# Dealing 24 modulation columns out among weight units, and reordering the opening of a two-layer decoder trunk

## Chip, cores and metric

One core of a Trainium2 chip runs the whole kernel. The metric is the device time of one execution in microseconds; where several were timed, the median is given.

## The reference, cut to what matters

A decoder trunk of two layers on one sequence of 1024 tokens, width 1024. Every layer takes six modulation vectors from the same condition: shift, scale and gate of the mixing half, shift, scale and gate of the MLP half.

```python
cond = jax.nn.silu(c)
for l in range(DEPTH):
    mod = cond @ w_mod[l] + b_mod[l]
    sh1, sc1, gt1, sh2, sc2, gt2 = [m[:, None, :] for m in jnp.split(mod, N_MOD, axis=-1)]
    h = rms_norm(x, norm_g[l, 0]) * (1.0 + sc1) + sh1
    y = mixer_block(h, positions, w_in[l], ...)
    x = x + gt1 * rms_norm(y, norm_g[l, 1])
    h = rms_norm(x, norm_g[l, 2]) * (1.0 + sc2) + sh2
    y = jnp.square(jax.nn.relu(h @ w_up[l])) @ w_down[l]
    x = x + gt2 * rms_norm(y, norm_g[l, 3])
```

`mixer_block` multiplies h by one input projection (2716 columns), feeds four mixers of width 256 from it (a short gated convolution, attention with a compressed, a full and a windowed branch, gated linear attention, a causal spatial gate over chunks of 128), norms each, and multiplies the four results by w_o. All matrices are fp32. Attention rotates 16 of its 64 dimensions by angles from `positions`.

## The kernel before, in words

Activations lie with features on the 128 partitions and 512 tokens along a tile, so a 1024-wide vector is eight tiles and the sequence is two halves (`hf` 0 and 1). A matrix product of fp32 is made of three TensorE matmuls at fp32r precision: weights and activations are each split into a high part (a cast, on ScalarE) and a low part (raw minus high, on VectorE: `sub`, L131), and `mm3` (L173 to L175) adds high by high, high by low, low by high into PSUM. A gemm (`gemm`) of one 128-wide output block is 24 such matmuls in two units of 12; `wunit` loads a unit's 256 KB (`wraw`, L158), casts it (L167) and subtracts (L131). Lanes are sets of buffers for this: "a" for w_o and the mixers, "b" for the second stream of the first half's mixing, "f" for the MLP. Lane "b" has three raw buffers of 256 KB and four for parts, so two units.

Work is ordered by a planner: the block is built with a scheduler that walks a simulated timeline, hands out buffers of a tag in turn, and gives each engine a fixed list; what comes earlier in the program has the higher priority, except where `tc.high_priority` moves it by an offset (the ones matmul of a norm, L195, forward). At run time every engine and every DMA-issuing queue takes its list in order. All loads and stores are issued by SyncE (SP).

Modulation vectors are not made by TensorE. `w_mod` is stored transposed, 128 outputs by 1024 inputs for each of 48 tiles of a layer; the condition is copied to all partitions (`cond`, 128x1024), and VectorE multiplies and sums along the row: `mod_dot` (L239) with a whole tile of 512 KB, `mod_half` (L247) with two halves of 256 KB and a small step that adds them and the bias. A column (j, k) is one such tile: modulation j, features 128k to 128k+127.

The opening (`start`) comes first: the rotary tables (`rope_tables`, tables of cosine and sine made with a chain of small VectorE steps, eight transposes and four matmuls, L380, and stored to DRAM), the condition's silu (L289 to L292), the loads of x, its norm factor R (`rms_R`: squares on ScalarE, L188 and L191, sums on VectorE, L137, one ones matmul, L195, then logarithm and exponential, L199 and L200), and then for each of eight k: columns (0, k) and (1, k), the tile of h (`make_h`: x by A1 and by R on VectorE, shift and cast on ScalarE, L209, low part on VectorE), and its 18 matmuls into six PSUM banks for the six input blocks `EARLY` (gates, compressed, full and window keys and values, queries). The six blocks' weights come in two halves (`wload` L277, `wsplit` L282), into a pool `kw` of their own.

`mix(0, 0)` then has its own order: a pool "wb" for lane "b", opened there; gates; attention (`nsa_part`) on lane "a"; linear attention (six gemms on lane "b"), spatial gate (four), convolution (six); then `mods_now`, which makes the 24 columns of modulations 2, 3 and 4 of layer 0 through lane "b"'s raw buffers; then attention's group norm, the split of the eight outputs, and the w_o gemms on lane "a" (`yo` copied by ScalarE, L946), beside which the second half's `norm` (its `make_h`) is made. Modulation 2 is needed by the residual after w_o, 3 and 4 by the next norm.

## Time and profile before

| | |
|---|---|
| median of 3 runs (lowest to highest) | 2634.32 us (2633.39 to 2635.1) |
| the profiled execution | 2634.88 us, span 2633.1 us |
| TensorE busy | 2488.4 us, 95% |
| VectorE busy | 1631.0 us, 62% |
| ScalarE busy | 1310.5 us, 50% |
| GpSimd busy | 53.0 us, 2% |
| granted TensorE clock, mean | 0.975 |
| moved by DMA | 305.79 MB, 116 GB/s |

Times of the profile count from the span's start. An engine is busy while an instruction runs on it; matmuls overlap, so a matmul's own duration is longer than its share of the queue. The granted clock is the share of TensorE's full clock that the chip allowed. "idle before <-releaser" tells how long an engine stood before an instruction and what it waited for last. DVE is VectorE, ACT ScalarE, POOL GpSimd, PE TensorE, PEld its weight loads, SP and SPq SyncE and its queue.

### The profile page before, as it was taken

To read this page: it belongs to the slowest core of one execution; us is meant where nothing else is said; L and a number is where in the kernel's file an instruction comes from. 1 tells how busy PE (TensorE), PEld (TensorE's weight loads), DVE (VectorE), ACT (ScalarE), POOL (GpSimd) and SP (SyncE) were. 2 spreads that over 40 slices of the span, in tenths; PEclk is the share of its full clock that TensorE was granted. 3 is DMA by queue.
4 is the path that set the end of the run, shared out by engine and by line. 5 is a ranking of instruction groups with operands and counts; after the bars stand their busy time and mean duration, and the time that the engine had idled before them with its cause. 6 is when DMAs were issued, how large, how long until landed. Compare 5 with 4: busy or idle time off the path is not lost.

```text
span 2633.1 us, 34406 instructions
## 1 busy us (share of the span) xinstructions
PE 2488.4 (95%) x11834; PEld 1987.3 (75%) x11834; DVE 1631.0 (62%) x3425; ACT 1310.5 (50%) x2657; POOL 53.0 (2%) x65
## 2 busy tenths in 40 slices
PE   5899499999999999999999999999999998899997
PEld 3666277777877878887787878877788876788886
DVE  7676866557888577444676476544567755634445
ACT  3573345445665356344366445444466744443333
POOL 0100000000000000000100000000100000000000
PEclk9899699999999999999999999999999999999999
DMA  8313634345434454322522344322322134433332
GB/s 279 100 46 100 203 117 132 106 140 153 129 123 134 155 164 140 102 85 89 154 83 70 116 152 140 99 84 79 119 77 68 57 108 143 136 97 96 97 97 75
DMA packets 176200, 305.79 MB, mean 116 GB/s; under 512 B 21573, under 2 KB 33434, under 8 KB 176026
## 3 DMA queue, kind: packets, MB, share of 16 engines
q1 hardware_dynamic: 176026, 303.60, 36.7%
q8 instruction: 93, 1.52, 0.2%
q14 instruction: 81, 0.66, 0.1%
HBM read 281.50 MB, written 17.83 MB: 114 GB/s over the span
## 4 chain that ended last, share of the span: by engine, by line
PE 83%; DVE 6%; DMA 4%; issue 1%; ACT 1%; POOL 0%; DVEq 0%; SPq 0%; ACTq 0%; POOLq 0%
PE ps_ff L173 16%; PE ps_ff L174 16%; PE ps_ff L175 16%; PE ps_mm L173 8%; PE ps_mm L175 8%; PE ps_mm L174 8%; DMA raw_f<-in_w_mod_dram 2%; PE ps_pv L783 1%; PE ps_mm L777 1%; PE ps_pv L782 1%; PE ps_s L822 1%; DMA raw_b<-in_w_mod_dram 1%; PE ps_s L824 1%; PE ps_t L777 1%; PE ps_t L195 1%
## 5 line engine op out<-in xcount | busy, mean ns | idle before, releaser
L167 ACT CAST w_f<-raw_f 128x512 fp32r<-128x512 f32 x504 | 311.7, 619 | 426.3 <-PE ps_ff L174 409.2
L131 DVE TENSOR_TENSOR w_f<-raw_f,w_f 128x512 fp32r<-128x512 f32 x504 | 350.4, 696 | 178.7 <-ACT w_f L167 167.9
L173 PE MATMUL ps_ff<-hid,w_f 128*128 128x512 f32 x992 | 395.4, 399 | 21.7 <-DVE yf L137 12.7
L175 PE MATMUL ps_ff<-h,w_f 128*128 128x512 f32 x1024 | 405.4, 396 | 1.2 <-DVE w_f L131 1.2
L173 PE MATMUL ps_ff<-h,w_f 128*128 128x512 f32 x1024 | 403.1, 394 | 0.0
L174 PE MATMUL ps_ff<-h,w_f 128*128 128x512 f32 x1024 | 402.3, 393 | 0.0
L174 PE MATMUL ps_ff<-hid,w_f 128*128 128x512 f32 x992 | 392.4, 396 | 1.5 <-DVE hid L131 1.5
L175 PE MATMUL ps_ff<-hid,w_f 128*128 128x512 f32 x992 | 391.7, 395 | 0.0
L173 PE MATMUL ps_mm<-h,w_a 128*128 128x512 f32 x784 | 318.2, 406 | 32.6 <-ACT yo L946 23.7
L175 PE MATMUL ps_mm<-h,w_a 128*128 128x512 f32 x784 | 317.2, 405 | 6.0 <-DVE w_a L131 6.0
L174 PE MATMUL ps_mm<-h,w_a 128*128 128x512 f32 x784 | 314.8, 403 | 3.6 <-DVE h L131 3.6
L167 ACT CAST w_a<-raw_a 128x512 fp32r<-128x512 f32 x196 | 121.3, 620 | 304.5 <-PE ps_mm L174 278.7
L131 DVE TENSOR_TENSOR w_a<-raw_a,w_a 128x512 fp32r<-128x512 f32 x196 | 135.1, 689 | 179.2 <-ACT w_a L167 173.3
L173 PEld LDWEIGHTS ps_ff<-hid,w_f 128*128 128x128 f32 x992 | 188.1, 190 | 69.8 <-DVE yf L137 15.2
L175 PEld LDWEIGHTS ps_ff<-h,w_f 128*128 128x128 f32 x1024 | 192.3, 188 | 45.5 <-issue 2.9
L173 PEld LDWEIGHTS ps_ff<-h,w_f 128*128 128x128 f32 x1024 | 192.4, 188 | 43.0 <-issue 3.1
L174 PEld LDWEIGHTS ps_ff<-h,w_f 128*128 128x128 f32 x1024 | 192.4, 188 | 42.0 <-issue 2.2
L174 PEld LDWEIGHTS ps_ff<-hid,w_f 128*128 128x128 f32 x992 | 188.3, 190 | 44.6 <-issue 2.9
L175 PEld LDWEIGHTS ps_ff<-hid,w_f 128*128 128x128 f32 x992 | 187.9, 189 | 41.1 <-issue 1.4
L137 DVE TENSOR_TENSOR y<-y,ps_ff 128x512 f32<-128x512 f32 (+1 forms) x208 | 138.0, 664 | 125.0 <-PE ps_ff L175 123.8
L173 PEld LDWEIGHTS ps_mm<-h,w_a 128*128 128x128 f32 x784 | 149.9, 191 | 72.8 <-ACT yo L946 24.1
L175 PEld LDWEIGHTS ps_mm<-h,w_a 128*128 128x128 f32 x784 | 149.8, 191 | 44.5 <-DVE w_a L131 7.7
(390 smaller groups left out, 3610.2 us busy)
## 6 DMA issues: line engine op xcount, KB each, us to landing
raw_f<-in_w_up_dram SPq DMA_DIRECT2D x256, 256.0 KB, 2.7
raw_f<-in_w_down_dram SPq DMA_DIRECT2D x256, 256.0 KB, 2.7
raw_a<-in_w_in_dram SPq DMA_DIRECT2D x132, 256.0 KB, 2.6
raw_f<-in_w_mod_dram SPq DMA_DIRECT2D x112, 256.0 KB, 2.9
raw_a<-in_w_o_dram SPq DMA_DIRECT2D x64, 256.0 KB, 2.7
raw_b<-in_w_mod_dram SPq DMA_DIRECT2D x48, 256.0 KB, 3.1
mw<-in_w_mod_dram SPq DMA_DIRECT2D x16, 512.0 KB, 5.7
bp<-in_cmp_w_dram SPq DMA_DIRECT2D x32, 256.0 KB, 5.7
```

The lines of the kernel that those rows point to most:

```text
L131: V.tensor_tensor(out=out, in0=a, in1=b, op=ALU.subtract)
L137: eng.tensor_tensor(out=out, in0=a, in1=b, op=ALU.add)
L167: A.copy(hi, raw)
L173: PE.matmul(ps_ap, wh, xh, start=start, stop=False)
L174: PE.matmul(ps_ap, wh, xl, start=False, stop=False)
L175: PE.matmul(ps_ap, wl, xh, start=False, stop=stop)
L195: PE.matmul(p, ones, acc, start=True, stop=True)
L777: PE.transpose(tp[0:kn, hh, :], cols(h0 + hh), ident)
L782: PE.matmul(pv[:, h0:h0 + nh, :], vst, th[0:kn], start=first[0], stop=False)
L783: PE.matmul(pv[:, h0:h0 + nh, :], vst, tl[0:kn], start=False, stop=last)
L822: PE.matmul(sp[:, 0:w], qh[:, h0 + hh, :], KX[:, 128 * k0:128 * k0 + w], start=True, stop=False)
L824: PE.matmul(sp[:, 0:w], ql[:, h0 + hh, :], KX[:, 128 * k0:128 * k0 + w], start=False, stop=True)
```

## The change

It has two parts. First, the 24 columns of modulations 2, 4 and 3 are taken out of their block behind the convolution: a generator yields one column after each weight unit of lane "b", and lane "b"'s pool is opened before `start`. Second, `start` is reordered: condition first, parameters and table inputs loaded from GpSimd's queue, first `w_mod` tiles ahead of x, six `w_mod` buffers instead of four, the sum of squares made by eight accumulating ones matmuls, x multiplied by R on GpSimd, scale and shift in one ScalarE step followed by a cast and a subtraction, the low parts of the early weights made on GpSimd and held in the ring of h tiles, the second half's early weights loaded at k = 1 and split at k = 3, and the rotary tables' arithmetic last, with another PSUM bank.

```diff
@@ -104,10 +104,10 @@
             d[name] = const.tile(shape, F32, name=f"{name}{l}")
         par.append(d)
 
-    def load_params(l, names):
+    def load_params(l, names, load=dma):
         src = {"ng": norm_g, "bmod": b_mod, "conv": conv_w, "gain": gains}
         for n in names:
-            dma(out=par[l][n], in_=src[n][l])
+            load(out=par[l][n], in_=src[n][l])
 
 
     KS = const.tile([128, 1024], F32R, name="KS")
@@ -169,6 +169,8 @@
         sub(lo, raw, hi.bitcast(F32))
         return hi, lo
 
+    beside = {}
+
     def mm3(ps_ap, wh, wl, xh, xl, start, stop):
         PE.matmul(ps_ap, wh, xh, start=start, stop=False)
         PE.matmul(ps_ap, wh, xl, start=False, stop=False)
@@ -177,6 +179,8 @@
     def gemm(ps_ap, lane, src, h, order=(0, 1, 2, 3, 4, 5, 6, 7)):
         for kh in (order[0] // 4, order[4] // 4):
             hi, lo = wunit(lane, src[:, 4 * kh:4 * kh + 4, :], [128, 4, 128])
+            if lane in beside:
+                next(beside[lane], None)
             for kk in order:
                 if kk // 4 == kh:
                     k = kk % 4
@@ -200,9 +204,9 @@
         A.activation(R, R, AF.Exp, scale=-0.5)
         return R
 
-    def make_h(xt, R, Ac, shc, ks=range(8)):
+    def make_h(xt, R, Ac, shc):
         h = []
-        for k in ks:
+        for k in range(8):
             t = nt()
             stt(t, xt[k], Ac[:, k:k + 1], R, ALU.mult, ALU.mult)
             hi, lo = htile(), htile()
@@ -265,10 +269,9 @@
     def start():
         d = par[0]
         early = {}
-        rope_tables()
-        with region("kw", "right") as kw, region("su") as su:
+        with region("kw", "right") as kw, region("rp") as rp, region("su") as su:
             def mk(src, shape):
-                t = su.tile(shape, F32, name="mw", tag="mw", bufs=4)
+                t = su.tile(shape, F32, name="mw", tag="mw", bufs=6)
                 dma(out=t, in_=src)
                 return t
 
@@ -278,48 +281,73 @@
                 return raw
 
             def wsplit(raw):
-                hi, lo = (kw.tile([128, 4, 128], F32R, name="w_k", tag="w_k", bufs=12) for _ in range(2))
+                hi, lo = (hp.tile([128, 4, 128], F32R, name="w_k", tag="h", bufs=32) for _ in range(2))
                 A.copy(hi, raw)
-                sub(lo, raw, hi.bitcast(F32))
+                P.tensor_tensor(out=lo, in0=raw, in1=hi.bitcast(F32), op=ALU.subtract)
                 return hi, lo
 
-            for hf in range(2):
+            def mload(k):
+                return [mk(w_mod[0, 8 * j + k], [128, 1024]) for j in (0, 1)]
+
+            halves = [slice(hf * T, hf * T + T) for hf in range(2)]
+            for c_ in halves:
+                dma(out=cond[:, c_], in_=c[:, c_].to_broadcast([128, T]))
+            load_params(0, ("ng", "bmod"), P.dma_start)
+            small = rope_loads(rp)
+            mws = {0: mload(0)}
+            xt = load_x(0)
+            raws = [wload(n, 0) for n in EARLY]
+            mws[1] = mload(1)
+            for c_ in halves:
                 t1, t2 = (su.tile([128, T], F32, name="ct", tag="ct", bufs=4) for _ in range(2))
-                ch = cond[:, hf * T:hf * T + T]
-                dma(out=ch, in_=c[:, hf * T:hf * T + T].to_broadcast([128, T]))
-                logsig(t2, ch, t1)
+                logsig(t2, cond[:, c_], t1)
                 A.activation(t2, t2, AF.Exp)
-                mul(ch, ch, t2)
-            xt = load_x(0)
-            load_params(0, ("ng", "bmod"))
-            R = rms_R(xt, 1.0 / 1024)
+                mul(cond[:, c_], cond[:, c_], t2)
+            p = ps("t")
+            for k in range(8):
+                sq = nt()
+                A.activation(sq, xt[k], AF.Square)
+                PE.matmul(p, ones, sq, start=k == 0, stop=k == 7)
+            R = rstd(p, 1.0 / 1024, su.tile([128, T], F32, name="R0"))
+            ws = {n: wsplit(r) for n, r in zip(EARLY, raws)}
+            for k in range(8):
+                mul(xt[k], xt[k], R, eng=P)
             bm = d["bmod"].rearrange("p (j k) -> p j k", k=8)
             hs = []
             for k in range(8):
                 ma = work.tile([128, 2, 1], F32, name="ma", tag="ma", bufs=4)
-                for j in (0, 1):
-                    mod_dot(0, j, k, mk, ma[:, j, :])
+                for j, raw in enumerate(mws.pop(k)):
+                    V.tensor_tensor_reduce(out=raw, in0=raw, in1=cond, scale=1.0, scalar=0.0,
+                                           op0=ALU.mult, op1=ALU.add, accum_out=ma[:, j, :])
                 add(d["mod"][:, 0:2, k:k + 1], ma, bm[:, 0:2, k:k + 1])
                 mod_scale(0, 1, slice(k, k + 1))
-                if k % 4 == 0:
-                    raws = [wload(n, k // 4) for n in EARLY]
-                hs += make_h(xt, R, d["A1"], d["mod"][:, 0, :], (k,))
-                if k % 4 == 0:
-                    ws = {n: wsplit(r) for n, r in zip(EARLY, raws)}
+                if k + 2 < 8:
+                    mws[k + 2] = mload(k + 2)
+                if k == 1:
+                    raws = [wload(n, 1) for n in EARLY]
+                t = nt()
+                A.activation(t, xt[k], AF.Identity, scale=d["A1"][:, k:k + 1], bias=d["mod"][:, 0, k:k + 1])
+                hs.append(split(t))
                 for i, n in enumerate(EARLY):
                     if k == 0:
                         early[n] = ps(("mm", "mm", "ff", "ff", "s", "s")[i])
                     hi, lo = ws[n]
                     mm3(early[n], hi[:, k % 4, :], lo[:, k % 4, :], hs[k][0], hs[k][1], k == 0, k == 7)
-        load_params(0, ("conv", "gain"))
-        load_params(1, ("ng", "bmod", "conv", "gain"))
+                if k == 3:
+                    ws = {n: wsplit(r) for n, r in zip(EARLY, raws)}
+            rope_tables(rp, *small)
+        load_params(0, ("conv", "gain"), P.dma_start)
+        load_params(1, ("ng", "bmod", "conv", "gain"), P.dma_start)
         return hs, early
 
     def mods_now(l, js, lane):
+
         for j in js:
             for k in range(8):
                 mod_half(l, j, k, lambda src, shape: wraw(lane, src, shape))
-            mod_scale(l, j, slice(0, 8))
+                if k == 7:
+                    mod_scale(l, j, slice(0, 8))
+                yield
 
     def mods_steps(todo, skip):
 
@@ -336,17 +364,20 @@
     cosd = dram.tile([2, 128, T], F32, name="cosd")
     sind = dram.tile([2, 128, T], F32, name="sind")
 
-    def rope_tables():
-        with region("rp") as rp:
+    def rope_loads(rp):
+        fr = rp.tile([128, 1, 8], F32, name="fr")
+        P.dma_start(out=fr, in_=freq.unsqueeze(0).to_broadcast([128, 1, 8]))
+        sl = rp.tile([17, 256], F32, name="sl")
+        P.dma_start(out=sl, in_=sel)
+        pi = rp.tile([128, 8, 1], I32, name="pi")
+        P.dma_start(out=pi, in_=pos.unsqueeze(2))
+        return fr, sl, pi
+
+    def rope_tables(rp, fr, sl, pi):
+        if True:
             def tk(n):
                 return rp.tile([128, 8, 8], F32, name=n)
 
-            fr = rp.tile([128, 1, 8], F32, name="fr")
-            dma(out=fr, in_=freq.unsqueeze(0).to_broadcast([128, 1, 8]))
-            sl = rp.tile([17, 256], F32, name="sl")
-            dma(out=sl, in_=sel)
-            pi = rp.tile([128, 8, 1], I32, name="pi")
-            dma(out=pi, in_=pos.unsqueeze(2))
             pf = rp.tile([128, 8, 1], F32, name="pf")
             V.tensor_copy(pf, pi)
             a, n, x2, sn, cs = tk("a"), tk("n"), tk("x2"), tk("sn"), tk("cs")
@@ -376,7 +407,7 @@
                 st = nt()[0:17]
                 A.copy(st.rearrange("p (j t) -> p j t", j=4), tp)
                 for w, dst in ((0, cosd), (128, sind)):
-                    p = ps("s")
+                    p = ps("pv")
                     PE.matmul(p, sl[:, w:w + 128], st, start=True, stop=True)
                     o = otile()
                     A.copy(o, p)
@@ -915,7 +946,8 @@
             gr = es.enter_context(region("gates"))
             if l == 0 and hf == 0:
                 sx = ("ff", "ff", "ff")
-                with region("wb", "right") as lane_pool["b"]:
+                with wbs:
+                    beside["b"] = mods_now(0, (2, 4, 3), "b")
                     with region("gl", "right") as rg:
                         gates, lrT = gate_part(l, hf, h, gr, rg, "a", early)
                         yn = nsa_part(l, hf, h, es.enter_context(region("ns")), gates, early)
@@ -923,7 +955,8 @@
                     with region("cv", "right") as rg, region("gm", "right") as rg2:
                         og = gmlp_part(l, hf, h, rg2, "b", sx)
                         oc = conv_part(l, hf, h, rg, "b", sx)
-                    mods_now(0, (2, 3, 4), "b")
+                    for _ in beside.pop("b"):
+                        pass
             else:
                 sx = ("s", "t", "pv")
                 with region("cv") as rg, region("gm") as rg2:
@@ -1056,6 +1089,8 @@
             xt.append(t)
         return xt
 
+    wbs = ExitStack()
+    lane_pool["b"] = wbs.enter_context(region("wb", "right"))
     h, early = start()
     xt = load_x(1)
     h = mix(0, 0, h, lambda: norm(0, 1, xt), early)
```

## Rows read from the trace of the kernel before

**Rows 1.** The page's busy line: us, share of span, instructions of each engine.

```profile
PE 2488.4 (95%) x11834; PEld 1987.3 (75%) x11834; DVE 1631.0 (62%) x3425; ACT 1310.5 (50%) x2657; POOL 53.0 (2%) x65
```

**Rows 2.** Windows by stage: length, busy us of each engine, granted clock, DMA share, GB/s.

```profile
8.75:40.00 31.25, 11.57 (x19) 3.67 (x19) 20.14 (x35) 16.64 (x31) 0.00 (x0) 1.00 0.97 334
40.00:75.20 35.20, 35.15 (x144) 28.13 (x144) 27.41 (x59) 10.55 (x18) 1.38 (x2) 1.00 0.74 249
75.20:102.80 27.60, 17.15 (x191) 15.11 (x192) 19.30 (x59) 13.27 (x46) 7.06 (x5) 0.68 0.28 77
102.80:176.00 73.20, 73.20 (x410) 57.74 (x410) 53.60 (x169) 53.30 (x139) 2.26 (x4) 0.98 0.21 62
176.00:210.00 34.00, 29.54 (x144) 19.31 (x143) 20.65 (x53) 20.10 (x50) 2.59 (x4) 0.95 0.08 28
210.00:256.00 46.00, 46.00 (x231) 36.66 (x229) 29.92 (x55) 17.13 (x33) 0.00 (x0) 1.00 0.32 102
256.00:319.29 63.29, 19.73 (x55) 12.29 (x55) 56.93 (x153) 23.16 (x39) 0.64 (x1) 0.63 0.64 202
```

**Rows 3.** Timeline around 319 us: start, us, engine, line, operation [idle before <-releaser].

```profile
318.04 0.72 ACT L209 ACTIVATE h<-nt,mod 128x512 fp32r<-128x512 f32 x1 [0.68 <-DVE nt L140]
...
318.67 1.05 ACT L946 COPY yo<-ps_mm 128x512 f32<-128x512 f32 x2
...
319.29 0.80 PE L173 MATMUL ps_mm<-h,w_a 128*128 128x512 f32 x1 [23.70 <-ACT yo L946]
```

**Rows 4.** Line 247's instructions from 240 to 330 us: ns min/median/max, first and last start.

```profile
L247 DVE CUSTOM_DVE_ANT_0 raw_b<-raw_b,cond x48: 680/685/695, 249.5 to 319.3; 128x512 f32<-128x512 f32 x48
...
  DMA raw_b<-in_w_mod_dram: 6.7, 12
```

**Rows 5.** Tile raw_b from 60 to 330 us: its loads' landing time, us.

```profile
L158 SPq DMA_DIRECT2D raw_b<-in_w_in_dram x32: 327/328/543, 73.8 to 243.8; - x32
...
DMA to landing us min/median/max: 2.4/3.0/4.1
```

**Rows 6.** Second lane, 244 to 246 us: matmuls three apart, a cast, a subtraction.

```profile
244.42 0.39 PE L173 MATMUL ps_mm<-h,w_b 128*128 128x512 f32 x1
...
245.08 0.62 ACT L167 CAST w_b<-raw_b 128x512 fp32r<-128x512 f32 x1 [2.05 <-PE ps_mm L174]
245.10 0.39 PE L173 MATMUL ps_mm<-h,w_b 128*128 128x512 f32 x1
...
245.73 0.69 DVE L131 TENSOR_TENSOR w_b<-raw_b,w_b 128x512 fp32r<-128x512 f32 x1 [1.99 <-ACT w_b L167]
```

**Rows 7.** Timeline of the opening, 26 to 41 us.

```profile
26.36 2.04 PE L195 MATMUL ps_t<-nt,ones 128*128 128x512 f32 x2 [5.61 <-DVE nt L137]
...
29.55 0.62 ACT L200 ACTIVATE nt<-nt 128x512 f32<-128x512 f32 x1
...
30.41 1.23 DVE L239 CUSTOM_DVE_ANT_0 mw<-mw,cond 128x1024 f32<-128x1024 f32 x1
...
40.00 1.22 PE L173 MATMUL ps_mm<-h,w_k 128*128 128x512 f32 x2 [11.59 <-ACT h L209]
```

**Rows 8.** Line 134's GpSimd instructions: ns min/median/max, first and last start us.

```profile
L134 POOL TENSOR_TENSOR p<-qs,cs x8: 1263/1292/1700, 81.3 to 1895.9; 128x512 f32<-128x512 f32 x8
```

**Rows 9.** VectorE, then GpSimd, from 78 to 84 us, in order of time.

```profile
79.52 1.64 DVE L131 TENSOR_TENSOR KW<-p,KW 64x512 fp32r<-64x512 f32 x1
81.19 2.36 DVE L131 TENSOR_TENSOR w_b<-raw_b,w_b 128x512 fp32r<-128x512 f32 x2
...
78.91 1.70 POOL L134 TENSOR_TENSOR p<-p,cs 128x512 f32<-128x512 f32 x1 [2.55 <-DVE p L664]
81.30 1.70 POOL L134 TENSOR_TENSOR p<-qs,cs 128x512 f32<-128x512 f32 x1 [0.69 <-DVE KW L131]
```

**Rows 10.** Line 380's matmuls: the rotary tables on TensorE.

```profile
L380 PE MATMUL ps_s<-nt,sl x8: 1056/1056/1217, 10.4 to 19.7; 17*128 17x512 f32 x8
```

**Rows 11.** Waits from 0 to 110 us: engine, line, releaser: us, times, longest.

```profile
PE ps_t L683 <- DVE gates L140: 4.8, 1, 4.8
```

## The prediction

> **What bounds the kernel now.** I read the page first: TensorE is busy for 2488.4 of 2633.1 us [rows 1], so 144.7 us of its idle time is all that a change of order can give back, plus what it runs at the lower clock. The windows by stage [rows 2] show where that lies. In 8.75 to 40 us it does 11.6 us of work and none of the real matmuls; in 40 to 75.2 it is full; in 75.2 to 102.8 it lacks 10.4 us; in 102.8 to 256 it lacks 4.5 us; in 256 to 319.29 it lacks 43.6 us, and its 19.7 busy us run at a granted clock of 0.63. These two holes, before 40 and after 256, are what the diff is about.
>
> The hole after 256 is read from its end. The timeline [rows 3] shows a w_o matmul that had waited 23.7 us for ScalarE's copy of `yo`, which stood in ScalarE's queue behind the bias step of `make_h` (L209), which waited for VectorE. What VectorE does there is line 247 [rows 4]: 48 half columns of `w_mod` from 249.5 to 319.3, one each 1.45 us although one takes 0.69, on a ring of three buffers. Group norms, splits and the next half's `make_h` are dealt between them, and VectorE is busy 56.9 of 63.3 us. So VectorE's order, fed by loads, ends last in that stage.
>
> **Part 1, the columns.** The same 48 loads and 48 reductions (24 columns of modulation 2, 4 and 3) are issued two at a time, after each of the first 24 of the 32 weight units of the second lane, and so behind that unit's load in SyncE's queue and its subtraction in VectorE's.
>
> What goes: at granted clock 1.0 the 19.73 busy us of the stage would be 0.63 x 19.73 = 12.4 us, so the stage holds 63.3 - 12.4 = 51 us that no matmul needs [rows 2]. What is late next is the last convolution gemm's tail: product, square, add, ones matmul, logarithm, exponential, gain, cast, subtraction, nine steps of 0.6 to 1 us, about 6.5 us. The w_o gemm starts with the other six inputs, 18 matmuls, which at 0.227 us each (three in 0.68, [rows 6]) hide 4.1 us. I leave 4 us exposed, since VectorE must now do the other 23 us of its work in that stage (56.9 less 44 half columns of 0.77 with their small steps) beside the w_o gemms. Gain: 51 - 4 = 47, between 41 and 51.
>
> What comes: 24 columns of 1.54 us, 37 us of VectorE, into 102.8 to 256 us. There VectorE is busy for 53.6 + 20.7 + 29.9 = 104.2 of 153.2 us [rows 2]; 49 us are free, and at 1.45 us each four half columns (3 us) lie before 256 already. Filled to 90%, it hides nearly all in total, but not everywhere: the ring has three buffers [rows 5], and where it held three weight loads ahead it now holds one weight and two half columns. For a weight to be in time, its load starts when the unit before it has been cast and subtracted (0.62 + 0.69, [rows 6]), lands 3.0 us later [rows 5], and is cast and subtracted in turn: 5.6 us after the gemm two units back began. Two units of 12 matmuls last 5.45 us. In the attention stretch, where a unit comes every 6 us, that is covered. In the twelve stepped units of the spatial and convolution parts, which run back to back, one reduction of 0.69 us ahead of it makes each late by about that: 12 x 0.7 = 8 us. Bounds: nothing (all hidden), and 34 us (all VectorE work ends up on the path). I take 8, because the stretch is TensorE's by the windows and the free time is larger than the load. On SyncE the 48 issues take 16 us of 153; behind one that waits for its buffer stand the copies of attention's query halves, which the next score matmuls need, and I count such waits within the 8.
>
> **Part 2, the opening.** Now the first real matmul starts at 40.0 [rows 7]. The row mean's chain ends at 30.2 (L200). The condition was loaded first but is ready only at 30.4, where the first 1.23 us reduction starts; ScalarE and VectorE had taken weight casts and squares ahead. From 30.4 VectorE works through 16 reductions, 16 normalising steps and subtractions.
>
> New chain: half a megabyte of condition, 1 MB of the first `w_mod` pair, 2 MB of x and 1.5 MB of weights at 334 GB/s [rows 2] are 15.7 us, after a landing time of 3 [rows 5]: the first weights are whole by 18.7, the first tile of x (1.75 MB) by 8.5. The sum of squares is now eight fp32 ones matmuls instead of one. One took 2.04 us [rows 7] from a standstill, so eight are at most 16.3 us from 8.5: R at some 26. GpSimd must first make six low parts, then multiply x by R. A two-operand instruction of this shape takes it 1.29 us [rows 8], against 0.69 on VectorE: six end at 27 if nothing disturbs them. But the two engines do not work side by side on such operands: at 79.52 VectorE needs 1.64 us for a half-size subtraction, and GpSimd's product that started at 78.91 takes 1.70 instead of 1.29; the next pair of VectorE subtractions takes 2.36 beside another 1.70 [rows 9]. They take turns. With a 1.22 us reduction between, six low parts end at 34. Then one product (1.3), scale and bias (0.7) and cast (0.6): the first matmul at 29.7 to 36.6, and I take 32, nearer the uncontended end, as two of the reductions are done before the weights land. **Gain 8 us at the start.** After it TensorE needs its 35.2 us as before [rows 2]. The rotary tables' matmuls, eight records of 1.06 us [rows 10], lay in the old hole; now they come after the sum of squares, at worst 8.5 us in the full stretch, at best in the wait for the first h. I take 2, which the warmer clock at the start gives back.
>
> The Trainium skill speaks against this part: GPSIMD Engine Reference, section 4.1, Engine selection, sends element-wise work on two tensors to VectorE because GpSimd is about two times slower, and section 1, Specifications, lists its SBUF interface as shared with VectorE instructions that read two SBUF inputs. The trace agrees on both (1.29 against 0.69; the stretched pairs). By it the opening would gain nothing, which is the first rival below.
>
> The check against that: reductions 16 x 1.22, low parts of h 8 x 0.69, GpSimd 20 x 1.29, condition, tables and small steps about 10, in all 61 us that cannot overlap; from 4 us on without a gap this ends at 65, and the last eighth of the matmuls (4.4) at 69.4, against 75.2 now. So the path ends at 65 to 78; 8 us gained, from 15 down to -3.
>
> Costed at nothing: eleven small parameter and table loads on GpSimd's queue. No row shows a load issued there; if each held it as long as a product (1.29), eleven end at 15 us, before it has weights to split, and SyncE's queue sheds as many; a gain from that is no more than the 0.33 us that an issue takes there [rows 5], eleven times. If the cover goes, the first h is later by what overruns. The second lane's pool opens earlier and `w_k` takes slots of the h ring, so four of the eight `cmp_w1` tiles wait for the end of the early gemms; they are then 2 or 3 us late, about what the earlier first `raw_b` loads give.
>
> **Sum.** 2634.9 (the profiled execution: span 2633.1 and 1.8 around it) - 47 + 8 - 8 = 2587.9. The median of the runs is 0.6 lower: 2587.
>
> **Rivals.**
> - *The opening gives nothing* (0.20): the turn-taking is complete and the tables fall on TensorE. For it: rows 9 and 61 us of such work. Against: VectorE sheds 8 normalising steps, 12 subtractions and 7 adds. 2634.3 - 47 + 8 = 2595, up to 2598.
> - *VectorE becomes the bound of the attention stretch* (0.15): 20 to 30 us instead of 8, as at 90% its queue delays softmax steps. For it: it is busy 73% of 102.8 to 176 as it is [rows 2], and the twelve columns of that part alone are 18 us against 19.6 free. Against: TensorE has the second lane's gemms to fill with. 2599 to 2609.
> - *More comes back* (0.12): TensorE waits 4.8 us for `gates` in 75.2 to 102.8 [rows 11], behind the two stretched `w_b` subtractions [rows 9], which can now be made in the opening; with the columns hidden wholly, 2574, at the extreme 2566.
> - *Slower* (0.05): the ring of three lets each stepped unit's weight load wait for a whole landing behind its two half columns. 24 x 3.0 = 72 us: 2634.3 - 47 - 8 + 72 = 2651. It decides from 55 / 24 = 2.3 us a unit. Against: that much is lost only if nothing else is ready for TensorE, and it is attention work that lies beside most units.
> - *The columns are not moved* (0.04): the scheduler leaves them last. The ring's order speaks against it, as a later weight's buffer is handed out after them. Then only the opening counts: 2626, or 2634 without it.
>
> **How the numbers follow.** The forecast has 0.44. About 0.2% (5 us) is what a measurement of this kernel can tell from no change. Faster takes the forecast, the first three rivals and half of the last: 0.93; same the other half, 0.02; slower 0.05. The range runs from the extreme of the third rival, 2566, to just past the second, 2612; outside lie the last two and tails.
>
> **What would show it.** Right: line 247's `raw_b` group spread over about 60 to 240 us, no `yo` wait above 5 us, the eight w_o gemms in about 50 us; the first `w_k` matmul at 30 to 36, the end of the early gemms near 67. Wrong: TensorE idle over 15 us between the first second-lane gemm and the last, with waits on `raw_b` loads or `w_b`; or GpSimd products of 1.7 us and more with the last low part of h after 68 us.

## The result, and the profile after

The changed kernel takes 2618.02 us (median of four, 2617.34 to 2619.75) against 2634.71 for the kernel before beside it (2633.39 to 2637.07): ratio 0.9937, 95% interval 0.9925 to 0.995. I had said 2587 us and a range of 2566 to 2612. The direction was right, the size was not, and the time lies outside the range. The profiled execution has a span of 2615.5 us, 17.6 less than before.

The windows by stage of the kernel after, to be read against [rows 2]. Columns are the stretch in us, its length, busy us (x instructions) of PE, PEld, DVE, ACT and POOL, granted clock, DMA share, GB/s.

```profile
8.75:40.00 31.25, 13.67 (x27) 6.65 (x28) 29.24 (x48) 12.29 (x21) 20.88 (x19) 0.78 0.95 345
40.00:76.50 36.50, 35.19 (x145) 27.15 (x144) 28.66 (x57) 15.21 (x25) 11.01 (x6) 0.95 0.63 210
76.50:113.00 36.50, 21.87 (x197) 16.44 (x197) 21.78 (x64) 14.58 (x48) 7.54 (x6) 0.65 0.39 121
113.00:280.40 167.40, 155.21 (x782) 115.83 (x781) 127.60 (x367) 90.75 (x222) 7.55 (x8) 0.95 0.38 115
280.40:343.80 63.40, 52.35 (x205) 39.58 (x204) 39.94 (x62) 37.29 (x64) 0.63 (x1) 0.89 0.32 100
```

The same view of the kernel before, for the stretch from the first to the last second-lane matmul and for what lies behind it up to the last copy of `yo`:

```profile
102.60:255.90 153.30, 148.84 (x781) 113.92 (x781) 104.25 (x274) 90.73 (x222) 4.85 (x8) 0.98 0.21 66
255.90:356.30 100.40, 56.84 (x205) 42.03 (x204) 70.88 (x176) 38.17 (x64) 0.64 (x1) 0.75 0.55 175
```

What moved is best read from four marks that both kernels have: the start of the last matmul of the early gemms, of the first and of the last second-lane matmul, and of the last copy of `yo`. The table gives them in us, for the experiments below too, with the three distances between them (gap: last early matmul to first second-lane matmul; stretch: first to last second-lane matmul; w_o: from there to the last `yo`). The marks come from one trace of each run. The five runs with the changed kernel's dealing have stretches of 165.9 to 169.3 us, so a difference of 2 or 3 us between two runs says little.

| run | ratio to before [interval] | early | first | last | yo | gap | stretch | w_o |
|---|---|---|---|---|---|---|---|---|
| before | 1 | 74.8 | 102.6 | 255.8 | 355.7 | 27.8 | 153.2 | 99.9 |
| **after** | 0.9937 [0.9925, 0.995] | 76.1 | 113.0 | 280.3 | 343.2 | 36.9 | 167.3 | 62.9 |
| cols_only | 0.9927 [0.9912, 0.9942] | 76.4 | 108.7 | 274.6 | 338.4 | 32.3 | 165.9 | 63.8 |
| open_only | 0.9997 [0.9987, 1.0006] | 74.8 | 109.2 | 263.0 | 359.8 | 34.4 | 153.8 | 96.8 |
| no_pool | 0.9915 [0.9897, 0.9934] | 69.9 | 103.9 | 271.6 | 334.7 | 34.0 | 167.7 | 63.1 |
| tables_first | 0.9919 [0.9904, 0.9934] | 80.9 | 107.5 | 276.8 | 339.8 | 26.6 | 169.3 | 63.0 |
| tables_first_no_pool | 0.988 [0.9865, 0.9896] | 70.8 | 96.2 | 263.6 | 326.7 | 25.4 | 167.4 | 63.1 |
| short_cols | 0.9915 [0.9901, 0.993] | 76.0 | 112.1 | 275.4 | 339.8 | 36.1 | 163.3 | 64.4 |
| no_col_loads | 0.9944 [0.993, 0.9959] | 76.2 | 109.5 | 281.8 | 345.5 | 33.3 | 172.3 | 63.7 |
| h_ring | 0.9962 [0.9948, 0.9976] | 74.9 | 109.3 | 286.2 | 350.0 | 34.4 | 176.9 | 63.8 |
| two_a_unit | 0.9981 [0.9972, 0.9991] | 77.2 | 119.0 | 287.7 | 351.4 | 41.8 | 168.7 | 63.7 |
| skip8 | 0.9946 [0.9931, 0.9961] | 74.5 | 108.7 | 278.6 | 342.4 | 34.2 | 169.9 | 63.8 |
| late16 | 0.9967 [0.9954, 0.998] | 75.9 | 110.1 | 277.6 | 348.8 | 34.2 | 167.5 | 71.2 |
| late16_tfnp | 0.9925 [0.9908, 0.9941] | 70.2 | 96.2 | 267.1 | 338.5 | 26.0 | 170.9 | 71.4 |
| late16_h | 0.9927 [0.991, 0.9943] | 75.2 | 109.2 | 274.6 | 339.4 | 34.0 | 165.4 | 64.8 |
| late16_short | 0.9945 [0.993, 0.9961] | 75.0 | 109.2 | 272.6 | 342.9 | 34.2 | 163.4 | 70.3 |
| late16_h_tfnp | 0.9877 [0.9862, 0.9892] | 70.6 | 96.3 | 262.1 | 326.6 | 25.7 | 165.8 | 64.5 |
| late24_h_tfnp | 0.989 [0.9872, 0.9908] | 70.6 | 96.3 | 255.8 | 328.0 | 25.7 | 159.5 | 72.2 |
| every2 | 0.9959 [0.9945, 0.9973] | 76.6 | 114.2 | 277.9 | 348.6 | 37.6 | 163.7 | 70.7 |
| every2_tfnp | 0.9913 [0.989, 0.9936] | 70.0 | 98.2 | 264.4 | 336.1 | 28.2 | 166.2 | 71.7 |

After against before: the opening ends 1.3 us later, the gap is 9.1 longer, the stretch 14.1 longer, the w_o stage 37.0 shorter, and another 5.1 us come after the last `yo`: -17.6. My sum had -8, 0, +8 and -47. No cause is shown for the 5.1: from the first matmul of the MLP to the next mixing's first `yo`, code that no edit touches, the traces take 450 to 459 us, and the kernel before has the 459.

**The w_o stage.** The hole went where it was to go. The group of line 251 (line 247 before, [rows 4]) in the trace of after is spread over 43 to 251 us. The view below is that of 60 to 310 us; the first two of the 48 half columns stand ahead of it, at 43 and 44 us:

```profile
L251 DVE CUSTOM_DVE_ANT_0 raw_b<-raw_b,cond x46: 659/688/694, 64.0 to 250.7; 128x512 f32<-128x512 f32 x46
  DMA raw_b<-in_w_mod_dram: 25.0, 15
```

(The first line gives shortest, median and longest in ns, the second how long VectorE stood before them for a load, and how often.) The 23.7 us wait for `yo` [rows 3] has no counterpart. Of what TensorE waited for from 280 to 345 the longest is 5.1 us for a cast of `h`. The timeline of that place (start, us, engine, line, operation, and in brackets the idle time before it and its releaser):

```profile
280.34 0.39 PE L177 MATMUL ps_mm<-h,w_b 128*128 128x512 f32 x1
280.77 0.69 DVE L134 TENSOR_TENSOR of<-of,ps_mm 128x512 f32<-128x512 f32 x1 [2.10 <-PE ps_mm L177]
287.20 1.80 ACT L226 CAST h<-of 128x512 fp32r<-128x512 f32 x3 [0.90 <-DVE of L140]
293.12 0.62 ACT L226 CAST h<-qs 128x512 fp32r<-128x512 f32 x1
293.79 0.80 PE L175 MATMUL ps_mm<-h,w_a 128*128 128x512 f32 x1 [5.09 <-ACT h L226]
```

From the convolution's last matmul to the first of w_o it is 13 us. w_o begins with attention's outputs (`qs`), and their group norm and casts stand behind the convolution's in ScalarE's list. This is read from the timeline; no run changes that order.

**The opening.** The first real matmul starts at 30.62 us, where I had said 32; the early gemms still end where they did. VectorE's timeline says why:

```profile
17.40 0.22 DVE L140 SCALAR_TENSOR_TENSOR sn<-sn,x 128x64 f32<-128x64 f32 x1
18.75 1.31 DVE L140 SCALAR_TENSOR_TENSOR sn<-sn,x 128x64 f32<-128x64 f32 x1
24.88 1.27 DVE L397 TENSOR_SCALAR cs<-cs 128x64 f32<-128x64 f32 x1
28.55 1.27 DVE L401 TENSOR_SCALAR sc<-n 128x64 f32<-128x64 f32 x1
29.73 2.33 DVE L320 CUSTOM_DVE_ANT_0 mw<-mw,cond 128x1024 f32<-128x1024 f32 x1
34.33 1.09 DVE L137 TENSOR_TENSOR mod<-ma,bmod 128x2 f32<-128x2 f32 x1
```

and GpSimd's, of the same time:

```profile
17.47 7.40 POOL L286 TENSOR_TENSOR w_k<-raw_k,w_k 128x512 fp32r<-128x512 f32 x6 [6.98 <-ACT w_k L285]
24.84 11.78 POOL L134 TENSOR_TENSOR y<-y,R 128x512 f32<-128x512 f32 x8
```

Until 17.47 a small step of the rotary tables takes 0.2 us; once GpSimd runs, each takes 1.3, one GpSimd instruction's time (six in 7.40 us), and ends 0.1 us after it. They stand in VectorE's list ahead of the second pair of columns, whose first reduction starts at 29.73 and takes 2.33 us instead of 1.22. What waited in the opening (us in all, times, longest):

```profile
ACT nt L329 <- DVE A L140: 29.0, 7, 9.1
PE ps_t L406 <- DVE sc L401: 9.4, 1, 9.4
PE ps_mm L176 <- DVE h L131: 6.2, 1, 6.2
```

ScalarE's scale and shift of h waited 29 us for the columns.

**The gap.** VectorE's timeline there:

```profile
80.18 0.69 DVE L251 CUSTOM_DVE_ANT_0 raw_b<-raw_b,cond 128x512 f32<-128x512 f32 x1 [8.09 <-DMA raw_b<-in_w_mod_dram]
85.06 0.69 DVE L251 CUSTOM_DVE_ANT_0 raw_b<-raw_b,cond 128x512 f32<-128x512 f32 x1 [3.52 <-DMA raw_b<-in_w_mod_dram]
85.79 0.68 DVE L685 COPY kvt<-ps_mm 64x512 f32<-64x512 f32 x1
```

and two lines of the waits from 76.5 to 113 us:

```profile
POOL p L134 <- DMA cs<-cosd: 28.1, 1, 28.1
DVE raw_b L251 <- DMA raw_b<-in_w_mod_dram: 11.6, 2, 8.1
```

Two dealt reductions stand ahead of the copy of the compressed keys (`kvt`) and wait for their loads: the first one's is issued at 73.57 us among eight tiles of `cmp_w1`, the second one's only at 80.91, behind the first reduction. And the tables' last matmuls (line 411) come only after the early gemms, at 76.46 to 81 us, so the table's load is issued at 81.76 and GpSimd's first rotation starts at 86.37 us instead of 73.82. (The 28 us are GpSimd's idle time before it; what counts is the later start.)

### The profile page after: what moved, and what is told of

Same layout as the page of the kernel before. It is cut to its first block, busy times and chain, and to the rows that moved or that the text cites. A ratio compares the mean times of both kernels' runs of the same rounds, so it can differ in the third digit from the quotient of the medians.

```text
span 2615.5 us, 34455 instructions
## 1 busy us (share of the span) xinstructions
PE 2493.0 (95%) x11848; PEld 1985.7 (76%) x11848; DVE 1633.1 (62%) x3398; ACT 1315.9 (50%) x2665; POOL 91.9 (4%) x96
## 4 chain that ended last, share of the span: by engine, by line
PE 81%; DVE 9%; DMA 6%; issue 2%; ACT 1%; SPq 0%; POOL 0%; DVEq 0%; ACTq 0%; POOLq 0%
PE ps_ff L175 16%; PE ps_ff L176 16%; PE ps_ff L177 16%; PE ps_mm L176 8%; PE ps_mm L177 8%; PE ps_mm L175 7%; DMA raw_f<-in_w_mod_dram 3%; DMA raw_b<-in_w_mod_dram 1%; PE ps_pv L814 1%; PE ps_mm L808 1%; PE ps_pv L813 1%; PE ps_t L199 1%; PE ps_t L808 1%; PE ps_s L853 1%; PE ps_s L855 1%
```

## The experiments

The first call for each part alone, for the opening, and for the stretch. Labels are those of the table.

**cols_only**: the first part of the change on the kernel before.

```diff
             hi, lo = wunit(lane, src[:, 4 * kh:4 * kh + 4, :], [128, 4, 128])
+            if lane in beside:
+                next(beside[lane], None)
...
-                    mods_now(0, (2, 3, 4), "b")
+                    for _ in beside.pop("b"):
+                        pass
```

> The kernel before with the columns dealt out alone; lane b's pool still opens behind the opening. Theory (the opening gives nothing, and the columns give about 42 in the w_o stage and take 14 back in the attention stretch): 2634.7 - 42 + 14 = 2607, 2602 to 2612. Rival A (the 9 us lost between the early gemms and the first second-lane gemm come with the columns too, as reductions that wait for their loads ahead of attention's steps): 2616. Rival B (all of the changed kernel's gain less a loss in the opening): under 2600.

**open_only**: the changed kernel with the columns back behind the convolution.

```diff
-                    beside["b"] = mods_now(0, (2, 4, 3), "b")
...
-                    for _ in beside.pop("b"):
+                    for _ in mods_now(0, (2, 3, 4), "b"):
```

> The changed kernel with the columns back in one block behind the convolution; the opening and the early pool of lane b stay. Theory (VectorE and GpSimd take turns, so the early gemms end no earlier than before, and the tables come late): 2634.7 + 1 to + 10 = 2636 to 2645. Rival A (the loss behind the early gemms is the columns'): 2630 to 2636. Rival B (the opening does save its 8 us and the columns hide it): 2625 to 2629.

The columns alone give 19.5 us (2612.3 against 2631.76), less than the 23 to 33 that their theory left and close to rival A's 19; the opening alone gives nothing: its interval holds 1, and its 2630.53 us lie in rival A's range. The windows of open_only, gap and stretch:

```profile
75.20:109.20 34.00, 24.72 (x197) 18.91 (x197) 19.54 (x59) 14.71 (x48) 8.01 (x6) 0.56 0.32 94
109.20:263.30 154.10, 149.66 (x782) 114.40 (x781) 104.50 (x275) 90.70 (x222) 4.84 (x8) 0.98 0.21 66
```

So the longer stretch belongs to the columns (153.8 without, 165.9 with them alone), and of the longer gap 6.6 us belong to the opening (34.4 against 27.8) and, in cols_only, 4.5 to the columns. In open_only VectorE's first step in the gap stands 9.8 us until one of the tables' matmuls of line 411 is done, and the copy of `kvt` starts at 81.49 us; with the two reductions in front of it, in the changed kernel, at 85.79. That the longer gap does not make open_only slower has no cause shown: 3.1 us come back in the w_o stage and 6.9 after the last `yo`, where the traces scatter as said.

**no_pool**: no arithmetic of the opening on GpSimd. **tables_first**: the tables' arithmetic ahead of everything, their inputs loaded by SyncE.

```diff
-                P.tensor_tensor(out=lo, in0=raw, in1=hi.bitcast(F32), op=ALU.subtract)
+                sub(lo, raw, hi.bitcast(F32))
...
-                mul(xt[k], xt[k], R, eng=P)
+                mul(xt[k], xt[k], R)
```

```diff
+            rope_tables(rp, *rope_loads(rp))
             halves = [slice(hf * T, hf * T + T) for hf in range(2)]
...
-            small = rope_loads(rp)
...
-            rope_tables(rp, *small)
```

> The changed kernel with the twelve low parts of the early weights and the eight products by R on VectorE instead of GpSimd. Theory (turn-taking: 20 GpSimd instructions of 1.29 us hold VectorE up, small steps take 1.3 instead of 0.2): VectorE takes on 20 x 0.69 = 14 us and sheds 26 us of waiting, so the early gemms end 5 to 12 us earlier: 2606 to 2613. Rival U (the w_mod loads set the pace): 2618, no change. Rival V (VectorE's own work sets it): 2618 + 14 = 2632.

> The changed kernel with the rotary tables' inputs loaded first from SyncE and their arithmetic ahead of everything else in start, as before the change; the rest stays. Theory: some nine small steps of 1.3 us in 17.5 to 29.8 go back to 0.2 each and the tables are in DRAM before attention asks for them, so the second column pair's reductions start up to 10 us earlier: 2604 to 2611. Rival (the GpSimd products and the loads set the pace anyway): 2615 to 2619.

**tables_first_no_pool**: both.

> Both edits of the opening: tables first, and no element-wise work on GpSimd. Theory (two separate costs of the opening: turn-taking, and tables that come late for attention): the first second-lane matmul at 95 to 100 us instead of 113, and the whole 10 to 15 us under the changed kernel, 27 to 32 under before. Rival (one and the same delay, shown twice): no better than either alone, 21 to 24 under before.

Both costs are real and add up, and the three times lie in their theories' ranges (tables_first narrowly: it is 20.9 us under the kernel beside it, where 24 to 31 were meant). Without GpSimd's arithmetic no 128x64 step of VectorE takes more than 0.24 us from 14 to 36 us, and the early gemms end 6.2 us sooner; with the tables first they end 4.8 later but the gap is 10.3 shorter; with both, the first second-lane matmul starts at 96.2 us, 16.8 sooner than in the changed kernel and 6.4 sooner than before. Ratio 0.988: this version beats both kernels. Its windows up to the second lane:

```profile
8.75:40.00 31.25, 22.92 (x40) 8.60 (x41) 26.32 (x63) 19.96 (x36) 0.00 (x0) 0.95 1.04 392
40.00:71.20 31.20, 31.20 (x138) 25.58 (x137) 23.42 (x57) 12.38 (x22) 0.85 (x1) 1.00 0.84 303
71.20:96.20 25.00, 16.22 (x191) 14.00 (x191) 18.46 (x57) 11.57 (x43) 8.56 (x6) 0.70 0.25 66
```

Its stretch, though, is the 167.4 us of the changed kernel. The rest is about that.

**short_cols**: each reduction over 8 elements. **no_col_loads**: no column loads; a tile of the h ring takes the result. **h_ring**: the loads go into tiles of the h ring instead of the weight ring.

```diff
-            V.tensor_tensor_reduce(out=raw, in0=raw, in1=cond[:, kh * T:kh * T + T], scale=1.0, scalar=0.0,
+            V.tensor_tensor_reduce(out=raw[:, 0:n], in0=raw[:, 0:n], in1=cond[:, kh * T:kh * T + n], scale=1.0, scalar=0.0,
...
-                mod_half(l, j, k, lambda src, shape: wraw(lane, src, shape))
+                mod_half(l, j, k, lambda src, shape: wraw(lane, src, shape), 8)
```

```diff
-            raw = mk(w_mod[l, 8 * j + k, :, kh * T:kh * T + T], [128, T])
-            V.tensor_tensor_reduce(out=raw, in0=raw, in1=cond[:, kh * T:kh * T + T], scale=1.0, scalar=0.0,
+            cs = cond[:, kh * T:kh * T + T]
+            raw = (mk(w_mod[l, 8 * j + k, :, kh * T:kh * T + T], [128, T]) if mk
+                   else hp.tile([128, T], F32, name="cx", tag="h", bufs=32))
+            V.tensor_tensor_reduce(out=raw, in0=raw if mk else cs, in1=cond[:, kh * T:kh * T + T], scale=1.0, scalar=0.0,
...
-                mod_half(l, j, k, lambda src, shape: wraw(lane, src, shape))
+                mod_half(l, j, k, None)
```

```diff
+    def mraw(src, shape):
+        raw = hp.tile(shape, F32, name="raw_m", tag="h", bufs=32)
+        dma(out=raw, in_=src)
+        return raw
...
-                mod_half(l, j, k, lambda src, shape: wraw(lane, src, shape))
+                mod_half(l, j, k, mraw)
```

> The changed kernel; each of the 48 dealt half columns is loaded whole as before, but VectorE multiplies and sums 8 of its 512 elements only, so the modulation values are not the reference's. The stretch from the first to the last second-lane matmul took 167.4 us in the changed kernel and 153 to 154 without the columns. Theory D (VectorE's time for the reductions makes the 14 us): it falls to 154 to 157, the whole to 16.7 + 12 = about 29 us under before. Theory L (the loads and the ring of three buffers make it): 164 to 168, whole within 4 us of the changed kernel, 16 to 20 under before.

> The changed kernel without the 48 loads of the dealt half columns: VectorE makes the same 48 reductions, but from the condition itself, into a free tile of the h ring, so the values are not the reference's. Theory D: the second-lane stretch stays at 164 to 168 and the whole gains only what VectorE waited behind the early gemms for two late loads (up to 8 us): 17 to 25 under before. Theory L: the stretch falls to 154 to 157, the whole 29 to 37 under before.

> The changed kernel with the dealt half columns loaded into tiles of the h ring (32 tiles, shared with attention's) instead of lane b's three raw buffers; loads and reductions unchanged. Theory L by the ring: weights are three loads ahead again, no wait for raw_b weight loads, the stretch 154 to 160: 24 to 31 under before. Theory D: 164 to 168, 14 to 20 under before.

Short reductions give back 4 of 14 us by this mark, nearer theory L's numbers than D's; what they give back apart from the clock comes below. The other two came out worse than the changed kernel, which neither theory had: no_col_loads makes its first reduction at 179.3 us, and h_ring at 181.9 (its first column load is issued at 178.1), by when the changed kernel has 31 of its 48 behind it. I take it that the tiles of the h ring came free no sooner; so the two runs did not unthrottle the columns but moved them into one burst. Windows of h_ring for the reductions alone (busy us of VectorE, granted clock, DMA share, GB/s):

```profile
180.00:200.00 20.00, 9.47 (x25) 0.86 0.76 238
200.00:220.00 20.00, 12.14 (x39) 0.63 0.81 264
220.00:240.00 20.00, 10.85 (x34) 0.71 0.56 183
```

and the windows of all its engines over its stretch:

```profile
109.30:286.40 177.10, 159.47 (x781) 118.99 (x781) 134.51 (x387) 91.14 (x221) 5.07 (x8) 0.89 0.39 121
```

The clock falls to 0.63 there, and attention's third block ends at 207 us instead of 198 in open_only, the fourth at 264 instead of 241. As tests of the ring they say little; that a burst costs more than dealing, they show.

Next, where and how densely the columns are dealt.

**two_a_unit**, **skip8**:

```diff
             if lane in beside:
                 next(beside[lane], None)
+                next(beside[lane], None)
```

```diff
-    def mods_now(l, js, lane):
+    def mods_now(l, js, lane, skip=8):
+        for _ in range(skip):
+            yield
```

> The changed kernel with two columns after each weight unit of the second lane instead of one, so that the 24 columns lie beside its first 12 units. Theory O (place): what costs 14 us between the first and the last second-lane matmul (167.4 us in the changed kernel, 153.3 before) is that the columns stand in VectorE's list where it is already busy two thirds of the time, beside the linear attention's first units; packed there twice as densely, the stretch grows to 172 to 182 us and the ratio to the kernel before to 0.9955 to 1.000. Theory W (work): the 37 us of reductions cost the same wherever they stand in the stretch; it stays at 165 to 170 us and the ratio at 0.993 to 0.995.

> The changed kernel with the dealing begun eight weight units later. Theory O: eight columns fewer stand in the crowded part, and the stretch falls to 158 to 163 us, ratio 0.989 to 0.992. Theory W: 165 to 170 us, ratio 0.993 to 0.995.

**late16** (skip 16, the rest beside w_o) and **late16_tfnp** (the same on tables_first_no_pool):

```diff
-                    for _ in beside.pop("b"):
-                        pass
+                    rest = beside.pop("b")
...
             y = []
+            if opening:
+                cur[0] = "a"
+                beside["a"] = rest
```

> The changed kernel with the dealing begun 16 units later (behind the linear attention's units), and the columns then left over dealt beside the w_o units of the first lane. Theory O: the stretch is 153 to 157 us as with the opening alone; the w_o stage takes in some ten columns, 15 us beside 23 us of its own VectorE work and 50 us of matmuls, and loses 0 to 4; ratio 0.988 to 0.991. Theory W: the stretch loses only the share of the ten columns, some 6 us of 14, and the w_o stage loses up to 4; ratio 0.991 to 0.994.

> The same late dealing on the version with the rotary tables first and without work on GpSimd, which gave 0.988. If place and opening add up (theory O): first second-lane matmul at 96 us, stretch 153 to 158 us in place of 167, ratio 0.983 to 0.986. Theory W: stretch 160 to 164 us, ratio 0.986 to 0.988.

Theory O (the place) falls: the stretch is 168.7, 169.9, 167.5 and 170.9 us. The ratio of two_a_unit is O's, but of the 12.0 us that its trace is longer than the changed kernel's 4.9 lie in the gap and only 1.4 in the stretch. Between these runs the gap moves with the pace of dealing: 34.2 with none dealt there (skip8, late16), 36.9 with one a unit, 41.8 with two. (It is not the pace alone: every2 below, with half of it, has 37.6.) Theory W fails for late dealing as well: fewer columns in the stretch, and it is no shorter. What late dealing does change is who waits. Attention's four blocks end (first copy of `qs`) at 130, 162, 202 and 248 us, near the 130, 162, 198 and 241 of open_only and not the 132, 171, 211 and 262 of the changed kernel; but the convolution's weight units come 4 to 5 us apart (the last eight in the changed kernel 2.5 to 4.3). And the w_o stage pays 8 us.

**late16_h**, **late16_short** (late dealing with the h ring, and with reductions over 8 elements), **late16_h_tfnp**, and **late24_h_tfnp** (skip 24):

```diff
-                mod_half(l, j, k, lambda src, shape: wraw(cur[0], src, shape))
+                mod_half(l, j, k, mraw)
```

```diff
-                mod_half(l, j, k, lambda src, shape: wraw(cur[0], src, shape))
+                mod_half(l, j, k, lambda src, shape: wraw(cur[0], src, shape), 8)
```

> The late dealing (begun behind the linear attention's 16 units, the rest beside w_o) with the half columns loaded into the ring of h tiles, so that they take no weight buffer. Late dealing alone gave a stretch of 167.5 us although the attention's blocks came back to the places that they have with the opening alone (130, 162, 202 us). Theory R (two prices: VectorE's list in the early place, the weight ring in the late place): without the weight ring the late place is nearly free, stretch 155 to 159 us, ratio 0.991 to 0.993. Theory W (the work costs the same 14 us wherever and on whatever ring): stretch 165 to 170 us, ratio 0.995 to 0.998.

> The late dealing with every reduction over 8 of its 512 elements (the rest of each column's sum is left out); loads, buffers and order as in late dealing. Theory R: what costs in the late place is the ring of weight buffers, not VectorE's time, so the stretch stays at 163 to 168 us. Theory V (VectorE's time in both places): the stretch falls to 155 to 159 us.

> Late dealing through the ring of h tiles, tables first, no work on GpSimd. Late dealing on this version had the first second-lane matmul at 96.2 us, the last at 267.1. Theory R: the last ends at 251 to 256 us and the ratio is 0.982 to 0.986 (0.988 with the dealing as in the changed kernel). Theory W: 263 to 269 us, ratio 0.990 to 0.993.

> The same with the dealing begun 24 units later, so that only eight columns at most lie ahead of w_o and 16 beside its units: 25 us of columns and 23 us of its own VectorE work on 50 us of matmuls. Theory R: stretch 153 to 156 us, and the w_o stage loses 3 to 10 us; ratio 0.982 to 0.988. Theory W: stretch 158 to 162 us, w_o stage as under R; ratio 0.985 to 0.991.

In the w_o stage the answer is plain: 71.2 us with the weight ring, 70.3 with the weight ring and almost no reduction time, 64.8 without the weight ring. There it is the ring. In the stretch theory R's number for late16_short came (163.4, 4 less) and its number for late16_h did not (165.4 instead of 155 to 159, which is theory W's): taking the ring away made a burst again, of 32 half columns from 181 to 219 us. The windows of late16_h:

```profile
190.00:220.00 30.00, 22.26 (x83) 13.43 (x82) 29.12 (x100) 12.20 (x31) 1.61 (x2) 0.72 0.69 226
```

VectorE is full and TensorE loses 7.7 of 30 us at a clock of 0.72. With 24 units skipped (late24_h_tfnp) the stretch is 159.5, theory W's number again, and the w_o stage 72.2, with 16 columns dealt beside it. late16_h_tfnp ends level with tables_first_no_pool (0.9877 and 0.988), between its two theories.

**every2**, **every2_tfnp**: one column after every second unit, the last eight beside w_o.

```diff
                     mod_scale(l, j, slice(0, 8))
                 yield
+                if cur[0] == "b":
+                    yield
```

> The changed kernel with one column after every second weight unit of the second lane (16 columns) and the other eight beside the first eight w_o units. Theory W (each column in the stretch costs about 0.6 us wherever it is dealt through the weight ring: 14 us for 24): stretch 160 to 163 us, w_o stage with 12 us of columns and 23 of its own work under 50 us of matmuls loses at most 3, ratio 0.990 to 0.993 (changed kernel 0.9937). Theory P (pace: it is only the density of one column a unit that costs): stretch 153 to 157 us, ratio 0.987 to 0.990.

> The same dealing on the version with the tables first and no work on GpSimd (0.988 with the dealing as in the changed kernel). Theory W: stretch 160 to 163 us, ratio 0.985 to 0.988. Theory P: stretch 153 to 157 us, ratio 0.982 to 0.985.

Theory P falls (163.7 and 166.2). Theory W's 160 to 163 is missed as well, narrowly by the first and by 3 us by the second, and both lose 8 us in the w_o stage, where W had at most 3.

**What the stretch's 14 us are.** From the two windows above: TensorE is idle for 167.40 - 155.21 = 12.2 us of it, before for 153.30 - 148.84 = 4.5. The other 6.4 us are busy time: as many matmuls, 155.21 us instead of 148.84, at a mean clock of 0.95 instead of 0.98. The granted clock has two levels here. At 0.50 matmuls start 0.43 us apart (297.19 and 297.62 in the changed kernel), at 1.00 0.23 (300.31 and 300.54). In the stretch TensorE is busy at 0.50 for 13.0 us, before for 6.4; half of the difference, 3.3 us, is what the lower clock costs. The other 3 I can place only in part: the work comes in 20 pieces instead of 10, and the matmul that ends a piece counts with its whole 0.39 us instead of 0.227, which is 1.6 us in all. So the 14.1 us are some 7.7 of idle time, 3.3 of clock and 3 of other busy time. In short_cols it is 7.9 idle and still 155.73 busy at 0.94:

```profile
112.10:275.70 163.60, 155.73 (x781) 117.64 (x781) 108.66 (x367) 89.60 (x221) 4.97 (x8) 0.94 0.38 118
```

There the clock alone makes the busy time longer: 21 us are at 0.50, which costs 7.3 us more than before. Apart from the clock the changed kernel's stretch is 10.8 us longer than before, and 9.1 to 10.5 in the four other runs with its dealing; that of short_cols is 2.8 us longer. So VectorE's time for the reductions is the larger part of it, some 8 us, as theory D had it, and in that one run the clock took 4 of the 8 back. VectorE also stands in front of reductions whose load has not landed, with the rest of its list behind them; in the changed kernel, from 113 to 280 us:

```profile
DVE raw_b L251 <- DMA raw_b<-in_w_mod_dram: 13.4, 13, 3.1
```

In short_cols it stands so for 26.1 us, and still only 2.8 are lost, so in this place it is not that wait. In the late place the same account gives 10.7 and 15.5 us through the weight ring (late16, late16_tfnp), 8.3 with short reductions and 6.4 and 6.3 through the h ring: there the weight ring seems to weigh more than the reductions' time, as theory R had it, though two traces of one dealing differ by 5 us.

What TensorE waited for in the changed kernel from 185 to 245 us is no one thing:

```profile
PE ps_pv L814 <- DVE w_a L131: 3.1, 5, 1.8
PE ps_t L808 <- DVE z L431: 1.9, 1, 1.9
PE ps_pv L813 <- ACT w_a L810: 1.8, 2, 1.2
PE ps_ff L633 <- POOL g L627: 1.2, 2, 0.9
```

The first three are matmuls and transposes of attention, the last is linear attention's, each released by one late step of VectorE, ScalarE or GpSimd. VectorE is busy 28.6 of 30 us just ahead of that, from 160 to 190 (22.1 before), and 46.8 of 60 from 185 to 245. Settled: the columns cause the 14 us; in the changed kernel's place some 8 of them go with the reductions' own time (one run) and 3.3 with the clock. Open: what the 2.8 are that short_cols leaves, and which order in VectorE's list would hide the 8. A lower priority for the columns was not tried.

## Why the prediction was off, by its own steps

- **"Gain 8 us at the start"** failed, although the first matmul came when predicted (30.62 for 32). I let turn-taking stretch the reductions and low parts, and counted "condition, tables and small steps about 10" in the sum of 61 us that cannot overlap. The tables' chain of 26 small steps alone held VectorE from 14.4 to 29.7 us, ahead of the second pair of columns, as the last ten of them waited for a whole GpSimd instruction each. no_pool shows that term at 6.2 us of early gemms. A sign that I gave for being wrong came: the last low part of `h` starts at 71.3 us (I had said after 68), with products of up to 2.3 us on GpSimd. The Trainium skill's GPSIMD Engine Reference, section 1, Specifications, speaks of VectorE instructions with two SBUF inputs or in a two-port mode; the trace agrees for the two-input steps down to 128x2 (1.09 us), and the one-input step at 24.88 (1.27 us) stretches alike, in a mode that no row here shows. The rival "the opening gives nothing" named the outcome, and open_only confirms it.
- **"I take 2"** for the tables' matmuls put them inside the early gemms, with a warmer clock at the start to give it back. The clock was 0.78 there, not the 1.00 of before [rows 2], and six of the matmuls' eight records came after the early gemms, and with them the table that GpSimd waited for. tables_first shows 10.3 us of gap. That nothing was counted between the early gemms and the second lane was the step left out: 9.1 us.
- **"I take 8"** for the columns in the stretch was a term of the right sign, within its bounds (0 and 34), and measured 14.1. The mechanism that I gave, stepped units late by a reduction each, shows only in late dealing; in the changed kernel it is attention's blocks that grow (39, 40 and 51 us apart, 32, 36 and 43 with the opening alone). That is the mechanism of the rival "VectorE becomes the bound of the attention stretch", at 14 us instead of its 20 to 30. I had also priced no clock there, which is 3.3 of the 14.
- **"I leave 4 us exposed"** in the w_o stage: the hole is gone as told, but the tail is 13 us. I counted the convolution's chain behind six other inputs that I took to be ready; attention's two were not, and w_o begins with them. To the last `yo` the stage gives 37.0 instead of 47, and the longer tail is 9 of the 10 us that are missing. The 5.1 us after the last `yo` I count to no step, as their cause is open.
- **Right:** `raw_b` spread from 43 to 251 us, no `yo` wait at all, the w_o gemms in 49.5 us from their first matmul to the last `yo`, the parameter loads on GpSimd's queue (0.53 to 0.73 us each, over at 9 us, ahead of its first product). The rival "slower" (a landing per unit) did not come: ScalarE waited 10.3 us in all for weight loads from 113 to 280.

Of the 29.4 us between the sum (-47) and the span's change (-17.6), 9.3 are the opening, 9.1 the gap, 6.1 the stretch and 10.0 the w_o stage; the 5.1 after the last `yo` go the other way.

## What to carry to other kernels

Before work is given to GpSimd, list everything that VectorE must do meanwhile, the smallest steps first: ten steps of 0.2 us took 12 us here. When work is moved beside a full engine, price the clock as well as the waits, take the clock's share out before two traces are compared, and look at what stands right behind each moved piece in its in-order queue. And after a hole is closed, ask which input the next stage begins with, since that chain is the new start.

## What was not expected of the hardware

A 128x64 step of VectorE went from 0.22 to 1.30 us, and an addition of two elements a partition took 1.09, while GpSimd worked on 128x512 operands. And small, scattered waits cost more than their length: in the stretch 7.7 us more of idle time went with 6.4 us more for the same matmuls, 3.3 of them by the granted clock, and in open_only's gap TensorE was busy for 24.72 us at a mean clock of 0.56, work of some 14 us at 1.00 (an estimate, 24.72 x 0.56).
